# A two-layer-mixer trunk on one core: the first norm's modulation taken as stationary blocks by TensorE

## The chip, the cores and the metric

The kernel runs on one core of one Trainium2 chip. The metric is the device time of one execution in microseconds. An engine is named as in the profile: PE is TensorE, with PEld its weight loads, DVE is VectorE, ACT is ScalarE, POOL is GpSimd, SP issues the transfers.

## The reference

One decoder layer with a mixer and a feed-forward part, each behind an RMS norm that is scaled and shifted by a conditioning vector c. What matters here is the head of it:

```python
c_act = jax.nn.silu(c)
mod = c_act @ w_mod[l] + b_mod[l]                      # (1, 6 * 1024)
sh1, sc1, gt1, sh2, sc2, gt2 = [m[:, None, :] for m in jnp.split(mod, N_MOD, axis=-1)]
h = rms_norm(x, norm_mix[l]) * (1.0 + sc1) + sh1
p = h @ w_in[l]
p_a, p_b, p_c = jnp.split(p, [P_A, P_A + P_B], axis=-1)
```

Behind it stand three kinds of heads on slices of p (a spatial gating unit, a gated linear recurrence, a delta-rule recurrence), the output projection, a second norm with sh2 and sc2, and a convolutional GLU of width 2816. The model width is 1024, the sequence 1024, all in f32.

## The kernel before

Channels lie on the 128 partitions (8 k tiles of the width), positions along the free axis in two halves of 512. A product in f32 precision is made as three products of rounded parts: each weight and each activation is split into a high part, a cast by ACT (L228), and a low part, the difference, by DVE or POOL (L229); then PE multiplies high by high, high by low and low by high.

The stage in question is the first norm of the first half, the part of `trunk` under the tile pool `st`. c goes through silu into `cs` (8 columns, L189 to L191). The squares of the 8 x tiles are summed into `sacc`; PE sums that over partitions with `ones` as the moving operand (`pss`), DVE makes the reciprocal root (`rsqrt`, 13 tiny operations), PE spreads it over the partitions (`pb`) and ACT copies it to `rb`.

The modulation is 12 groups of 512 outputs. The order of w_mod's columns is such that groups 0 to 3 hold shift and scale of the first norm, each group for two k tiles of h. A group's weights come as four blocks `wm` of 512 KB, with two k tiles each. In groups 0 to 3 the eight k tiles are shared: ACT scales k tiles 0 to 3 by their column of `cs` and POOL adds them (`mod_ap`, into the first `mb`); DVE scales and adds k tiles 4 to 7 (`mod_v`, into the second `mb`). `mod_fin` then lets PE sum both `mb` over the partitions, in 4 + 4 matmuls with an `mb` slice as stationary operand and one column of ones as moving operand, into a PSUM tile `pm`; DVE adds the bias (`modc`) and makes the gain (`sg1`, named `sg` in the profile).

Of each group's two tiles of h, DVE multiplies x by gain and `rb` (`h_hi`; for k tiles 4 to 7 POOL has multiplied by `rb` already, `xr`), ACT adds the shift and rounds to the high part (h00h to h07h), DVE takes the low part (`h_lo`, h00l to h07l). Three weight tiles of w_in (`ws`, split into wh_s and wl_s) are multiplied as their h tiles come: `prod(k1, i1)` makes all products up to k tile k1 of the first i1 weight tiles, each once, into `pf`. The rest of w_in follows in later lines with `load_w` and `gemm`.

The order on each engine is that of the program's text wherever the wrapper `Ordered` is on (`V.on` and its like). It is on for DVE, ACT and POOL through this stage, and for PE around `mod_fin` and `prod` (`TON`). SP issues transfers in the text's order; each waits until its buffer is free (6 buffers of `wm`, 3 of the raw w_in tile). Behind the stage comes a row of small operations on `spt` (a softplus of 3 columns by series, L457 to L476), mostly on POOL, ACT's two parts of it behind h07h in ACT's queue.

Of the kernel before, what the change touches and what calls it, by code (L numbers as in the profile page):

```python
# [10 lines left out]
F32 = mybir.dt.float32  # L11
F32R = mybir.dt.float32r
I32 = mybir.dt.int32
AF = mybir.ActivationFunctionType
ALU = mybir.AluOpType
# [3 lines left out]
P = 128  # L19
D = 1024  # L20
S = 1024
H = 512
# [32 lines left out]
NF2 = 3  # L55
NT2, NTB, _ = 7, 9, 5
NWR, NWL, NH = 3, 2, 16
NAP, NXV, NFIRST, TON, XRO = (4, 4, 4, 4), 4, 3, True, ((4, 4), (4, 6), (6, 8), (8, 8))
VPIN = 0
ENG = {'s2':'G','KB1': 'V',  # L60
 'S1': 'V',
# [88 lines left out]
def trunk(ctx: ExitStack, tc: tile.TileContext, xT, wmod, w_in, w_out, w_up, w_down,  # L150
          par, const, sgu_ln, sgu_wT, sgu_b, lora, g2w, lruw, outT):
    nc = tc.nc
    V, A, G, T = (Ordered(tc, e) for e in (nc.vector, nc.scalar, nc.gpsimd, nc.tensor))
# [70 lines left out]
    def eng(key, d):  # L224
        return {"V": V, "G": G, "A": A}[ENG.get(key, d)]

    def split(src, hi, lo, e=None):
        A.copy(hi, src)  # L228
        (e or V).tensor_tensor(lo, src, hi.bitcast(F32), ALU.subtract)  # L229
# [100 lines left out]
    with tc.tile_pool(name="st", bufs=1, reuse_waits="tile") as st:  # L330
        xs, ws = [], []

        def mod_load(m):
            for k2 in range(KT // 2):
                wt = st.tile([P, 2, H], F32, tag="wm", name=f"wm{m}_{k2}", bufs=6)
                SY.dma_start(wt, wmod[m, k2])
                wm[m] += [wt[:, 0, :], wt[:, 1, :]]
            mb[m] = [st.tile([P, H], F32, tag=f"mb{i}", name=f"mb{m}{i}", bufs=2) for i in range(2)]

        def mod_ap(m):  # L340
            a = mb[m][0]
            for k in range(NAP[m]):
                A.activation(wm[m][k] if k else a, wm[m][k], AF.Copy, scale=cs[:, k:k + 1])
                if k:
                    G.tensor_tensor(a, a, wm[m][k], ALU.add)

        def mod_v(m, k0, k1):
            a = mb[m][1]
            for k in range(max(k0, NAP[m]), k1):
                if k == NAP[m]:  # L350
                    V.tensor_scalar(a, wm[m][k], cs[:, k:k + 1], None, ALU.mult)
                else:
                    V.scalar_tensor_tensor(a, wm[m][k], cs[:, k:k + 1], a, ALU.mult, ALU.add)

        def mod_fin(m):
            ps = mp.tile([P, H], F32, tag="m", name=f"pm{m}")
            for n, a in enumerate(mb[m]):
                for i in range(4):
                    T.matmul(ps[:, i:i + 1], a[:, i * P:(i + 1) * P], ones, start=(n == 0 and i == 0), stop=(n == 1),
                             skip_group_check=True)  # L360
            V.tensor_tensor(modc[:, 4 * m:4 * m + 4], ps[:, 0:4], col("b_mod", 4 * m, 4), ALU.add)
            V.scalar_tensor_tensor(sg1[:, 2 * m:2 * m + 2], modc[:, 4 * m + 1:4 * m + 4:2], 1.0,
                                   col("norm_mix", 2 * m, 2), ALU.add, ALU.mult)

        def w_load(i):
            raw, hi, lo = ws[i]
            SY.dma_start(raw, w_in[i].rearrange("p k c -> p (k c)"))

        def h_hi(k):
            x, sh = xs[k], modc[:, 2 * k:2 * k + 1]  # L370
            if k < NXV:
                V.scalar_tensor_tensor(x, x, sg1[:, k:k + 1], rb, ALU.mult, ALU.mult)
            else:
                V.tensor_scalar(x, x, sg1[:, k:k + 1], None, ALU.mult)
            A.activation(hs[k][0], x, AF.Identity, bias=sh)

        def h_lo(k):
            V.scalar_tensor_tensor(hs[k][1], xs[k], modc[:, 2 * k:2 * k + 1], hs[k][0].bitcast(F32),
                                   ALU.add, ALU.subtract)

        def xr(k0, k1):
            for k in range(k0, k1):
                G.tensor_tensor(xs[k], xs[k], rb, ALU.mult)

        wm, mb = [[] for _ in range(4)], [None] * 4
        hs = [htile(f"h0{k}") for k in range(KT)]
        acts[0] += hs
        for i in range(NFIRST):
            raw = wp.tile([P, 1024], F32, tag="wraw", name=f"wr_s{i}", bufs=NWR)
            hi = st.tile([P, 1024], F32R, tag=f"wsh{i}", name=f"wh_s{i}")  # L390
            lo = st.tile([P, 1024], F32R, tag=f"wsl{i}", name=f"wl_s{i}")
            ws.append((raw, hi, lo))
            first[i] = acp.tile([P, H], F32, tag="acc", name=f"pf{i}")

        done = [0] * NFIRST

        def prod(k1, i1):
            for k in range(k1):
                ah, al = hs[k]
                for i in range(min(i1, NFIRST)):  # L400
                    if done[i] == k:
                        hi, lo = (t.rearrange("p (k c) -> p k c", c=P)[:, k, :] for t in ws[i][1:])
                        T.matmul(first[i], hi, ah, start=(k == 0), stop=False)
                        T.matmul(first[i], hi, al, start=False, stop=False)
                        T.matmul(first[i], lo, ah, start=False, stop=(k == KT - 1))
                        done[i] += 1

        V.on = A.on = G.on = True
        sacc = st.tile([P, H], F32, name="sacc0")
        for k in range(KT):  # L410
            xk = st.tile([P, H], F32, tag=f"x{k}", name=f"x0{k}")
            SY.dma_start(xk, xT[k * P:(k + 1) * P, 0:H])
            sq = st.tile([P, H], F32, tag="sq", name=f"sqx{k}", bufs=2)
            A.activation(sacc if k == 0 else sq, xk, AF.Square)
            if k:
                V.tensor_tensor(sacc, sacc, sq, ALU.add)
            xs.append(xk)
        mod_load(0)
        mod_load(1)
        mod_ap(0)  # L420
        rb = sumsq_bcast([sacc], mp, st, "rb", "n10", 1)
        mod_v(0, 0, 8)
        w_load(0)
        mod_load(2)
        w_load(1)
        mod_load(3)
        if NFIRST == 3:
            w_load(2)
        SY.dma_start(cst, const[:, 0:C_ID])
        lraw = wp.tile([P, 1024], F32, tag="wraw", name="lraw", bufs=NWR)[:, 0:768]  # L430
        SY.dma_start(lraw, lora.rearrange("p a b -> p (a b)"))
        for m in range(4):
            if m < 3:
                mod_ap(m + 1)
                mod_v(m + 1, 0, 6)
            xr(*XRO[m])
            T.on = TON
            mod_fin(m)
            if TON:
                prod(2 * m, m)  # L440
            T.on = False
            h_hi(2 * m)
            h_hi(2 * m + 1)
            if m < 3:
                mod_v(m + 1, 6, 8)
            h_lo(2 * m)
            h_lo(2 * m + 1)
            if m < NFIRST:
                split(*ws[m], eng(f"s{m}", "V"))
        prod(KT, NFIRST)  # L450
        V.on = A.on = G.on = False

    r2 = r2s.enter_context(tc.tile_pool(name="r2", bufs=1, reuse_waits="tile"))
# [950 lines left out]
```

## Time and profile before

| what | value |
|---|---|
| median of 3 runs | 1389.36 us (1388.76 to 1389.72) |
| the profiled execution | 1389.59 us |
| its span | 1387.8 us |
| PE busy in the span | 1256.2 us (91%) |
| DVE, ACT, POOL busy | 914.4, 584.0, 413.3 us |
| PE busy, 30 to 62.2 us | 19.50 of 32.20 us |
| DVE busy, 30 to 62.2 us | 31.65 of 32.20 us |

A view by windows gives, for each stretch of the span, its length, the busy time of each engine with the number of instructions, then the granted clock of TensorE as a share of 2.4 GHz, the DMA share and GB/s. A timeline row is start, duration (of the whole row), engine, line, operation, tiles and count; in brackets the idle time ahead of it and what ended it. Line L146 is the wrapper `Ordered`, so rows of this stage are told apart by their tiles. Buffer numbers are left out: `wm` is any of its blocks. An f32 matmul has two records, so a row of x8 is four matmuls.

### The profile page before, as it was taken

Reading aid. Unit: us, or ns where it says so; the run is one execution under the profiler, and the core shown is the slowest. Engines: PE = TensorE matmul, PEld = TensorE weight load, DVE = VectorE, ACT = ScalarE, POOL = GpSimd, SP = SyncE. Lnnn points to the kernel's source line nnn. Section 1 sums busy time; section 2 is a strip of 40 time slices with the busy share of each in tenths; the row PEclk is TensorE's granted clock in tenths of the full one; section 3 lists DMA queues with packets and bytes.
Section 4 is the critical chain, followed back from the end, with each engine's and each line's share of the span. In section 5 each row is a group of like instructions: output and inputs, shape, how many; then the busy total and the mean of one; then the engine's idle time right before and its main releaser. Section 6 shows DMA issues by size and latency. Waiting matters only on the chain. (4 is left out here: it accounts for less than half of the span.)

```text
span 1387.8 us, 18658 instructions
## 1 busy us (share of the span) xinstructions
PE 1256.2 (91%) x6948; PEld 1025.9 (74%) x6948; DVE 914.4 (66%) x1624; ACT 584.0 (42%) x1008; POOL 413.3 (30%) x337
## 2 busy tenths in 40 slices
PE   2778999978898979989878999999999999999996
PEld 2566878667686867768656778888888888888885
DVE  7968776765668584567898766666666575332566
ACT  3454654854655366333444334343343342110231
POOL 5683423306124220023466433323333200000000
PEclk9999999979999988899989999999999999999998
DMA  6554161433314243385412322222222374321213
GB/s 225 189 168 121 35 168 52 113 126 97 83 51 109 65 124 107 116 272 188 137 45 84 100 91 84 91 84 91 74 71 91 109 261 133 93 76 51 82 54 121
DMA packets 87498, 153.89 MB, mean 111 GB/s; under 512 B 37616, under 2 KB 39280, under 8 KB 87408
## 3 DMA queue, kind: packets, MB, share of 16 engines
q1 hardware_dynamic: 87408, 152.71, 35.3%
q8 instruction: 54, 0.88, 0.3%
q14 instruction: 36, 0.29, 0.1%
HBM read 126.60 MB, written 26.08 MB: 110 GB/s over the span
## 5 line engine op out<-in xcount | busy, mean ns | idle before, releaser
L1246 DVE SCALAR_TENSOR_TENSOR x<-pd,modc,x 128x512 f32<-128x512 f32 x80 | 59.5, 748 | 83.4 <-PE pd L248 83.3
L1293 POOL TENSOR_TENSOR x<-x,rb_n 128x512 f32<-128x512 f32 x2 | 3.0, 1520 | 218.2 <-ACT rb_n L270 218.2
L287 POOL TENSOR_TENSOR macc<-macc,wm 128x512 f32<-128x512 f32 x35 | 46.8, 1338 | 68.1 <-ACT wm L285 66.0
L228 ACT CAST wh_wd<-wr_wd 128x768 fp32r<-128x768 f32 (+2 forms) x32 | 21.7, 677 | 93.6 <-PE pd L247 92.2
L229 POOL TENSOR_TENSOR wl_wo<-wr_wo,wh_wo 128x1024 fp32r<-128x1024 f32 x9 | 22.0, 2445 | 113.3 <-DVE O L774 57.6
L1224 POOL TENSOR_TENSOR u<-u,g 128x512 f32<-128x512 f32 x21 | 27.7, 1321 | 92.6 <-ACT g L1147 92.6
L229 DVE TENSOR_TENSOR wl_ug<-wr_ug,wh_ug 128x1024 fp32r<-128x1024 f32 x22 | 28.9, 1318 | 34.3 <-ACT wh_ug L228 34.3
L755 DVE TENSOR_SCALAR U<-q,rn 128x64 f32<-128x64 f32 x48 | 13.4, 279 | 48.3 <-PE q L743 41.1
L624 PE MATMUL pg<-KGd,KB 128*128 128x128 f32 x192 | 31.1, 307 | 7.5 <-DVE KGd L609 5.0
L763 ACT COPY O<-q 128x64 f32<-128x64 f32 x48 | 10.1, 211 | 65.5 <-PE q L743 65.2
L228 ACT CAST wh_ug<-wr_ug 128x1024 fp32r<-128x1024 f32 x22 | 23.1, 1052 | 34.2 <-PE pA L1122 31.3
L743 PE MATMUL q<-SS,KGd 128*128 128x64 f32 x180 | 36.7, 287 | 0.0
L743 PE MATMUL q<-VV,SCd 128*128 128x64 f32 x192 | 35.0, 285 | 0.3
L1208 DVE TENSOR_TENSOR p<-p,pB 128x512 f32<-128x512 f32 x21 | 14.4, 685 | 31.0 <-PE pB L1123 31.0
L1147 ACT ACTIVATE g<-g 128x512 f32<-128x512 f32 x44 | 27.9, 634 | 14.8 <-DVE g L1142 14.8
L624 PEld LDWEIGHTS pg<-KGd,KB 128*128 128x128 f32 x192 | 27.2, 215 | 9.0 <-DVE KGd L609 5.7
L228 ACT CAST wh_wo<-wr_wo 128x1024 fp32r<-128x1024 f32 x16 | 16.7, 1047 | 38.8 <-PE po L247 30.9
L743 PEld LDWEIGHTS q<-VV,SCd 128*128 128x128 f32 x192 | 29.9, 202 | 4.1 <-ACT O L763 1.4
L1140 DVE SCALAR_TENSOR_TENSOR g<-pA,pr,g 128x511 f32<-128x511 f32 (+1 forms) x42 | 31.2, 742 | 2.4 <-ACT g L1138 2.2
L1140 DVE SCALAR_TENSOR_TENSOR g<-p,pr,g 128x511 f32<-128x511 f32 (+1 forms) x42 | 32.1, 764 | 0.9 <-ACT g L1138 0.9
L285 ACT ACTIVATE wm<-wm,cs 128x512 f32<-128x512 f32 x35 | 24.1, 718 | 15.3 <-DMA wm<-in_wmod_dram 9.3
L1201 POOL TENSOR_TENSOR wr_ug<-wr_ug,wr_uv 128x512 f32<-128x512 f32 x18 | 29.7, 1651 | 1.4
(5041 smaller groups left out, 4574.1 us busy)
## 6 DMA issues: line engine op xcount, KB each, us to landing
wm<-in_wmod_dram SPq DMA_DIRECT2D x48, 512.0 KB, 4.1
wr_ug<-in_w_up_dram SPq DMA_DIRECT2D x22, 512.0 KB, 3.6
wr_uv<-in_w_up_dram SPq DMA_DIRECT2D x22, 512.0 KB, 3.6
wr_g<-gd SPq DMA_DIRECT2D x22, 512.0 KB, 3.5
x<-in_xT_dram SPq DMA_DIRECT2D x32, 256.0 KB, 5.2
wr_wo<-in_w_out_dram SPq DMA_DIRECT2D x16, 512.0 KB, 4.3
wr_wd<-in_w_down_dram SPq DMA_DIRECT2D x16, 384.0 KB, 3.0
gd<-c SPq DMA_DIRECT2D x21, 256.0 KB, 2.0
```

Source lines behind the costliest of these rows:

```text
L228: A.copy(hi, src)
L229: (e or V).tensor_tensor(lo, src, hi.bitcast(F32), ALU.subtract)
L285: A.activation(acc if k == 0 else wt[:, j, :], wt[:, j, :], AF.Copy, scale=cs[:, k:k + 1])
L287: G.tensor_tensor(acc, acc, wt[:, j, :], ALU.add)
L624: T.matmul(pg[hh][:, c, :, :], KB[:, 4 * g + c, :, :].rearrange("p a b -> p (a b)"), KG[g][:, c, :, r_], start=True, stop=True)
L743: T.matmul(o, w, x, start=start, stop=True, skip_group_check=True)
L1140: V.scalar_tensor_tensor(g[:, d:H], src[:, 0:H - d], taps[2 - d], g[:, d:H], ALU.mult, ALU.add)
L1147: A.activation(g, g, AF.Silu)
L1201: eng("S4" + e, "G").tensor_tensor(g1, g1, v1, ALU.subtract)
L1208: V.tensor_tensor(self.p1, self.p1, psB, ALU.add)
L1224: eng("c22", "V").tensor_tensor(u3, u3, g1_, ALU.mult)
L1246: V.scalar_tensor_tensor(x, ps, modc[:, 40 + k:41 + k], x, ALU.mult, ALU.add)
```

## The change

In groups 0 to 3 PE takes blocks of w_mod itself. `mod_pe` uses a 128 x 128 block of `wm` as stationary operand and the fitting column of `cs` as moving operand, four matmuls for each k tile, all into the group's `pm`. Group 0 does so for all eight k tiles, the first four ahead of `pss` and the others behind `pb`. In groups 1 to 3 PE takes k tiles 4 to 7, and DVE scales and adds k tiles 0 to 3 into one `mb`, which PE adds with `ones` as before. `mod_ap` is gone, and with it all work of POOL and ACT on the blocks. POOL now multiplies all eight x tiles by `rb`, ACT multiplies them by the gain, and POOL takes the low parts of all three first weight tiles (before, DVE took two). `wm` has 8 buffers instead of 6. PE is in program order through the whole stage.

```diff
+        def mod_pe(m, k0, k1, end=False):
+            if m not in pms:
+                pms[m] = mp.tile([P, H], F32, tag="m", name=f"pm{m}")
+                fresh.add(m)
+            src = [(wm[m][k], cs[:, k:k + 1]) for k in range(k0, k1)]
+            if end and mb[m] is not None:
+                src.append((mb[m], ones))
+            for n, (w, x) in enumerate(src):
+                for i in range(4):
+                    T.matmul(pms[m][:, i:i + 1], w[:, i * P:(i + 1) * P], x, start=m in fresh,
+                             stop=end and n == len(src) - 1, skip_group_check=True)
+                    fresh.discard(m)
...
         def h_hi(k):
             x, sh = xs[k], modc[:, 2 * k:2 * k + 1]
-            if k < NXV:
-                V.scalar_tensor_tensor(x, x, sg1[:, k:k + 1], rb, ALU.mult, ALU.mult)
-            else:
-                V.tensor_scalar(x, x, sg1[:, k:k + 1], None, ALU.mult)
+            A.activation(x, x, AF.Copy, scale=sg1[:, k:k + 1])
             A.activation(hs[k][0], x, AF.Identity, bias=sh)
...
-        mod_ap(0)
-        rb = sumsq_bcast([sacc], mp, st, "rb", "n10", 1)
-        mod_v(0, 0, 8)
...
+        T.on = True
+        mod_pe(0, 0, 4)
+        rb = sumsq_bcast([sacc], mp, st, "rb", "n10", 1)
+        mod_pe(0, 4, 8, True)
+        mod_v(1, 0, 4)
+        xr(0, 4)
+        mod_fin(0)
         for m in range(4):
-            if m < 3:
-                mod_ap(m + 1)
-                mod_v(m + 1, 0, 6)
-            xr(*XRO[m])
-            T.on = TON
-            mod_fin(m)
-            if TON:
-                prod(2 * m, m)
-            T.on = False
             h_hi(2 * m)
             h_hi(2 * m + 1)
             if m < 3:
-                mod_v(m + 1, 6, 8)
+                mod_pe(m + 1, 4, 8, True)
             h_lo(2 * m)
             h_lo(2 * m + 1)
-            if m < NFIRST:
-                split(*ws[m], eng(f"s{m}", "V"))
+            if m < 3:
+                mod_fin(m + 1)
+                if m < 2:
+                    mod_v(m + 2, 0, 4)
+                split(*ws[m], eng(f"s{m}", "G"))
+                xr(*((4, 6), (6, 8), (8, 8))[m])
+                prod(2 * m + 2, m + 1)
         prod(KT, NFIRST)
```

PE's queue from its start, before: `pss` is first, and a group is two rows of four matmuls.

```order
L255 MATMUL pss_n_221<-ones,sacc_154 128x1 x4
L266 MATMUL pb_n_241<-ident,rsq_n_228 128x128 x4
L146 MATMUL pm_287<-ones,mb_202 128x1 x4
L146 MATMUL pm_287<-ones,mb_203 128x1 x4
L146 MATMUL pm_319<-ones,mb_212 128x1 x4
L146 MATMUL pm_319<-ones,mb_213 128x1 x4
L146 MATMUL pf_145<-h00h,wh_s_143 128x512
```

The same place after the change: 16 matmuls of group 0 stand ahead of `pss`, 16 behind `pb`, and group 1 has 16 + 4 ahead of the first product.

```order
L146 MATMUL pm_232<-cs,wm_0_194 128x1 x8
L146 MATMUL pm_232<-cs,wm_1_196 128x1 x8
L146 MATMUL pss_n_249<-ones,sacc_154 128x1 x4
L146 MATMUL pb_n_269<-ident,rsq_n_256 128x128 x4
L146 MATMUL pm_232<-cs,wm_2_198 128x1 x8
L146 MATMUL pm_232<-cs,wm_3_200 128x1 x8
L146 MATMUL pm_307<-cs,wm_2_206 128x1 x8
L146 MATMUL pm_307<-cs,wm_3_208 128x1 x8
L146 MATMUL pm_307<-ones,mb_292 128x1 x4
L146 MATMUL pf_145<-h00h,wh_s_143 128x512
```

Groups 2 and 3 have the same 16 + 4 matmuls ahead of 18 and of 48 products. ACT's queue at the end of the stage, before (the x tiles come scaled from DVE):

```order
L146 ACTIVATE h06h<-x_184,modc 128x512
L146 ACTIVATE h07h<-x_189,modc 128x512
L146 ACTIVATE spt<-pr 128x3
L228 CAST wh_r_610<-wr_r_608 128x1024
L146 ACTIVATE spt<-spt 128x3
```

And after, where ACT scales each x tile ahead of the h tile that is made from it:

```order
L146 ACTIVATE x_184<-x_184,sg_77 128x512
L146 ACTIVATE h06h<-x_184,modc 128x512
L146 ACTIVATE x_189<-x_189,sg_77 128x512
L146 ACTIVATE h07h<-x_189,modc 128x512
L146 ACTIVATE spt<-pr 128x3
L228 CAST wh_r_637<-wr_r_635 128x1024
L146 ACTIVATE spt<-spt 128x3
```

POOL's queue of the stage, after; before, 12 adds of blocks stood in it, four products by `rb` and the split of the third weight tile only.

```order
L146 TENSOR_TENSOR x_155<-x_155,rb_n_274 128x512
L146 TENSOR_TENSOR x_159<-x_159,rb_n_274 128x512
L146 TENSOR_TENSOR x_164<-x_164,rb_n_274 128x512
L146 TENSOR_TENSOR x_169<-x_169,rb_n_274 128x512
L146 TENSOR_TENSOR wl_s_144<-wr_s_142,wh_s_143 128x1024
L146 TENSOR_TENSOR x_174<-x_174,rb_n_274 128x512
L146 TENSOR_TENSOR x_179<-x_179,rb_n_274 128x512
L146 TENSOR_TENSOR wl_s_148<-wr_s_146,wh_s_147 128x1024
L146 TENSOR_TENSOR x_184<-x_184,rb_n_274 128x512
L146 TENSOR_TENSOR x_189<-x_189,rb_n_274 128x512
L146 TENSOR_TENSOR wl_s_152<-wr_s_150,wh_s_151 128x1024
```

All rows behind the stage stand in the same order as before on every engine, SP's from its first to its last.

## Rows read from the trace of the kernel before

**Rows 1.** Windows of the span, busy by engine, with granted clock before DMA share

```profile
30.00:62.20 32.20, 19.50 (x76) 16.19 (x77) 31.65 (x33) 12.00 (x17) 21.11 (x14) 0.98 0.62 231
...
24.85:30.13 5.28, 5.28 (x24) 5.19 (x24) 3.13 (x5) 3.04 (x5) 1.27 (x1) 1.00 0.46 117
49.52:53.94 4.42, 4.42 (x12) 3.40 (x13) 4.35 (x5) 0.93 (x2) 4.26 (x3) 1.00 0.44 118
53.94:60.90 6.96, 4.44 (x27) 3.57 (x25) 6.82 (x7) 2.38 (x3) 4.91 (x4) 0.99 0.01 4
61.77:67.60 5.83, 5.83 (x14) 4.57 (x15) 4.93 (x10) 3.41 (x6) 1.58 (x2) 0.50 0.30 90
67.60:75.24 7.64, 7.64 (x34) 5.96 (x32) 0.89 (x3) 2.27 (x4) 5.52 (x25) 1.00 0.46 144
65.72:86.02 20.30, 17.92 (x77) 14.14 (x76) 7.37 (x9) 9.09 (x17) 17.65 (x44) 0.95 0.66 210
...
546.00:556.00 10.00, 9.25 (x41) 8.75 (x41) 3.09 (x8) 6.68 (x12) 0.00 (x0) 0.50 0.00 0
```

**Rows 2.** Timeline of PE in the first stage

```profile
18.95 1.84 PE L255 MATMUL pss_n<-ones,sacc 128*128 128x1 f32 x8 [18.95 <-DVE sacc L146]
24.85 2.08 PE L266 MATMUL pb_n<-ident,rsq_n 128*128 128x128 f32 x8 [4.06 <-DVE rsq_n L146]
26.72 3.41 PE L146 MATMUL pm<-ones,mb 128*128 128x1 f32 x16
...
55.80 0.95 PE L146 MATMUL pm<-ones,mb 128*128 128x1 f32 x8
...
74.85 0.39 PE L405 MATMUL pf<-h07h,wl_s 128*128 128x512 f32 x1
```

**Rows 3.** Timeline of DVE, first stage and what follows it

```profile
13.25 0.17 DVE L191 TENSOR_TENSOR cs<-cs,pr 128x8 f32<-128x8 f32 x1
...
21.02 0.79 DVE L146 TENSOR_SCALAR rsq_n<-rsv_n 128x4 int32<-128x4 int32 x1
...
21.92 1.24 DVE L146 TENSOR_SCALAR rsq_n<-rsv_n 128x4 f32<-128x4 f32 x1
...
24.63 0.16 DVE L146 SCALAR_TENSOR_TENSOR rsq_n<-rsq_n 128x4 f32<-128x4 f32 x1
...
62.19 0.15 DVE L146 TENSOR_TENSOR modc<-pm,pr 128x4 f32<-128x4 f32 x1
...
86.05 1.22 DVE L572 TENSOR_TENSOR_SCAN cc<-scanm,sg 128x512 f32<-128x512 f32 x1 [5.75 <-POOL sg L570]
```

**Rows 4.** Timeline of ACT at the end of the first stage

```profile
63.79 0.70 ACT L146 ACTIVATE h07h<-x,modc 128x512 fp32r<-128x512 f32 x1
```

**Rows 5.** Timeline of POOL behind the first stage

```profile
65.72 1.17 POOL L146 TENSOR_SCALAR spt<-spt 128x3 f32<-128x3 f32 x1 [4.00 <-ACT spt L146]
...
85.40 0.62 POOL L570 TENSOR_SCALAR sg<-sg 128x512 f32<-128x512 f32 x1
```

**Rows 6.** Groups of equal instructions, 12 to 66 us: count, busy us, mean ns, idle before

```profile
L146 POOL TENSOR_TENSOR mb<-mb,wm 128x512 f32<-128x512 f32 x12 | 18.0, 1496 | 20.7 <-ACT wm L146 20.1
...
L146 DVE SCALAR_TENSOR_TENSOR mb<-wm,cs,mb 128x512 f32<-128x512 f32 x12 | 11.7, 972 | 0.3
...
L146 ACT ACTIVATE wm<-wm,cs 128x512 f32<-128x512 f32 x12 | 7.7, 706 | 0.0
L146 POOL TENSOR_TENSOR x<-x,rb_n 128x512 f32<-128x512 f32 x4 | 5.6, 1429 | 0.0
...
L146 ACT CAST wh_s<-wr_s 128x1024 fp32r<-128x1024 f32 x3 | 3.1, 1028 | 0.0
...
L146 POOL TENSOR_TENSOR wl_s<-wr_s,wh_s 128x1024 fp32r<-128x1024 f32 x1 | 2.6, 2553 | 2.0 <-ACT wh_s L146 2.0
```

**Rows 7.** Groups of PE instructions, 540 to 556 us

```profile
L743 PE MATMUL q<-VV,SCd 128*128 128x64 f32 x16 | 4.8, 398 | 0.1
```

**Rows 8.** DMA issues on the page: count, KB each, median us to landing

```profile
wm<-in_wmod_dram SPq DMA_DIRECT2D x48, 512.0 KB, 4.1
```

More of the change, by code (lines that the diff above doesn't have):

```diff
@@ L57 @@
 NWR, NWL, NH = 3, 2, 16
-NAP, NXV, NFIRST, TON, XRO = (4, 4, 4, 4), 4, 3, True, ((4, 4), (4, 6), (6, 8), (8, 8))
+NFIRST = 3
 VPIN = 0
@@ L334, in mod_load @@
             for k2 in range(KT // 2):
-                wt = st.tile([P, 2, H], F32, tag="wm", name=f"wm{m}_{k2}", bufs=6)
+                wt = st.tile([P, 2, H], F32, tag="wm", name=f"wm{m}_{k2}", bufs=8)
                 SY.dma_start(wt, wmod[m, k2])
                 wm[m] += [wt[:, 0, :], wt[:, 1, :]]
[L338 to L345, printed above, removed]
@@ L347, in mod_v @@
         def mod_v(m, k0, k1):
[L348 to L351, printed above, removed]
-                else:
-                    V.scalar_tensor_tensor(a, wm[m][k], cs[:, k:k + 1], a, ALU.mult, ALU.add)
-        def mod_fin(m):
[L356 to L360, printed above, removed]
+            for k in range(k0, k1):
+                if k == 0:
+                    mb[m] = st.tile([P, H], F32, tag="mb", name=f"mb{m}", bufs=2)
+                    V.tensor_scalar(mb[m], wm[m][k], cs[:, k:k + 1], None, ALU.mult)
+                else:
+                    V.scalar_tensor_tensor(mb[m], wm[m][k], cs[:, k:k + 1], mb[m], ALU.mult, ALU.add)
@@ L361, in mod_fin @@
+        def mod_fin(m):
+            ps = pms[m]
             V.tensor_tensor(modc[:, 4 * m:4 * m + 4], ps[:, 0:4], col("b_mod", 4 * m, 4), ALU.add)
@@ L383, in xr @@
                 G.tensor_tensor(xs[k], xs[k], rb, ALU.mult)
-        wm, mb = [[] for _ in range(4)], [None] * 4
+        wm, mb, pms, fresh = [[] for _ in range(4)], [None] * 4, {}, set()
         hs = [htile(f"h0{k}") for k in range(KT)]
@@ L426, in trunk @@
         mod_load(3)
-        if NFIRST == 3:
-            w_load(2)
+        w_load(2)
         SY.dma_start(cst, const[:, 0:C_ID])
@@ L444, in trunk @@
             if m < 3:
-                mod_v(m + 1, 6, 8)
+                mod_pe(m + 1, 4, 8, True)
             h_lo(2 * m)
             h_lo(2 * m + 1)
-            if m < NFIRST:
-                split(*ws[m], eng(f"s{m}", "V"))
+            if m < 3:
[5 more added lines that the diff above has]
+                prod(2 * m + 2, m + 1)
         prod(KT, NFIRST)
+        T.on = False
         V.on = A.on = G.on = False
```

## The prediction

> **What bounds the kernel now.** The change touches only the first norm, so I read that stage first, then what leaves it. From 30 to 62.2 us DVE is busy 31.65 of 32.20 us and PE 19.50 [rows 1]: there DVE is the limit, because it sums half of the modulation, scales x and splits weights. PE stands behind it: its small matmuls with `ones` run in bits of four and eight [rows 2]. The last of the four modulation groups reaches `modc` at 62.19 [rows 3]. Behind that hang ACT's h06h and h07h, then the two `spt` activations [rows 4], then a chain of small operations on POOL that starts at 65.72 and goes on without a real pause (17.65 us busy of 20.30) to `sg` at 85.40 [rows 1, 5]. DVE waited 5.75 us for exactly that and goes on at 86.05 [rows 3]. PE's last first-stage product starts at 74.85 [rows 2]. So what the change is worth is read from one moment: when the fourth `modc` can be computed. All instructions behind the stage stand in the same order on all five engines before and after; so I take the shift of that moment to reach the end one to one.
>
> **The change, part by part.** Removed: 12 adds on POOL (1496 ns each), 16 ACT scalings (12 of the `wm` kind at 706 ns), and on DVE 16 of the 972 ns kind become 12 [rows 6]; DVE also loses the scaling of x (to ACT, with POOL's product by `rb` before it) and two of three weight splits (to POOL). Added: 60 matmuls of one column on PE, 92 instead of 32. With this DVE has nothing left that fills the stage; the question is PE, which now works in program order and must do all of it before each group of h tiles.
>
> The price of such a matmul: eight of them in a row (16 records, an f32 matmul has two) took 3.41 us from 26.72, so 0.426 each; four (8 records) took 0.95 us from 55.80, so 0.24 (I use 0.25) [rows 2]. The difference is the clock: before 53.94 PE is at 1.2 GHz (that column of the view has no reading until its first change, so I go by the spacing), then 2.4 GHz until 60.90, 1.2 GHz (0.50) until 67.60, then 2.4 [rows 1]. The 512-column products take 5.83/14 = 0.42 us at the lower level (I use 0.43) and 7.64/34 = 0.225 at the upper [rows 1].
>
> Which level will hold? 5.28 us of unbroken small matmuls from 24.85 did not end in the upper clock; 4.42 us and 5.83 us of 512-column products did (49.52 to 53.94, 61.77 to 67.60) [rows 1]. And much later, from 546 to 556, f32 matmuls of 64 columns fill 9.25 of 10 us and the clock stays at 0.50 throughout [rows 1, 7]. So I take 1.2 GHz for the new matmuls wherever no run of 512-column products goes ahead. The Trainium skill ("TensorE: Matmul & The Clock Gate", Part 1, the HAM clock gate) says otherwise: sustained activity releases the clock, as a matter of time and not of the number of matmuls. By that rule the long new stretch would run at 2.4 GHz; the stretch at 546 does not agree, and the case is a rival below.
>
> Now PE's list, on the axis of the profiled execution:
> - First half of group 0: from `cs` (13.25 + 0.17, say 13.5 [rows 3]) 16 × 0.426 = 6.8, to 20.4 (a 512 KB block lands 4.1 us after its issue [rows 8], and these are asked for before any other weights). It stands ahead of `pss`, which began at 18.95 [rows 2]; so `pss` is 1.45 late and ends at 22.2.
> - DVE's rsqrt chain took from 20.79 to 24.79, with two tiny operations stretched to 0.79 and 1.24 us (0.16 is usual) [rows 2, 3] while POOL's adds ran. Those adds are gone. If the stretching goes too (about 1.7 us), `pb` starts at 24.6; if not, at 26.2. Nearest to the row's own operations without it is the first; with a little for gaps I take 24.85, as before.
> - `pb` 1.87 (24.85 to 26.72 [rows 2]); second half of group 0, 6.8, to 33.5; group 1 (16 + 4), 8.5, to 42.0; six products 2.7, to 44.7; group 2, 8.5, to 53.2.
> - Eighteen products: the upper clock comes after 4.42 or 5.83 us of them, so 4.42 + 7.7 × 0.225 = 6.2 or 5.83 + 4.4 × 0.225 = 6.8; I take 6.6, to 59.8.
> - Group 3: after its first rise the upper clock lasted 7 us (53.94 to 60.90 [rows 1]) though small matmuls and waits filled much of it. From a rise at about 58.4 that reaches to 65, so 20 matmuls at 0.25, 5.0, to 64.8. At the lower level it would be 8.5.
>
> Does PE wait for anything in between? The nearest case is POOL's split of the first weights, needed at about 42.5. `modc` of group 0 is ready at 33.6; ACT's four operations on x and h and the cast (1028 ns [rows 6]) take to 38, the split 2.55 us (2553 ns [rows 6]), to 40.4; POOL's four products by `rb` (1429 ns each [rows 6]) are done by 33.3. That leaves 2 us. The blocks of groups 2 and 3 that wait for PE's reading are asked for at 30 to 42 and wanted 10 us later or more, against 4.1 us to land [rows 8]. So PE is unbroken from 24.85 on, and is the limit.
>
> The fourth `modc` then comes at 64.8 against 62.19: **2.6 us later**. Behind it ACT now does four operations, each pair dependent, about 2.85 us (0.71 each [rows 6]) plus 0.35 for `modc` and its gain; before, h07h ended at 63.79 + 0.70, 2.3 us after `modc` [rows 3, 4]. That is another **1.0 us**. POOL's chain starts 3.6 us later. PE's own 48 remaining products: 5.8 us at the lower level (13.6 of them), then 34.4 × 0.225 = 7.7, so to 78.3 against 75.24, 3.1 late: the two meet as before. Sum: +3.6 us.
>
> The profiled execution took 1389.59 us (span 1387.8 and 1.8 around it), the median of the runs shown is 1389.36; from the median, **1393.0**. What a measurement of this kernel can tell from no change is about 0.2%, 2.8 us; the sum lies a little beyond.
>
> **Rivals.**
> - *The clock rises in the small matmuls* (faster). If they raise it as the products from 49.52 did, 4.42 us after the unbroken run begins at 24.85, that is at 29.3. Group 0 then ends at 31.8, group 1 at 36.8; PE waits for the first split to 38.7; group 2 ends at 44.8, the eighteen products at 49.0, group 3 at 54.0. `modc` comes 8.2 us earlier, less the 1.0 on ACT: -7.1, **1382**. It decides from the point where a small matmul in the second half of group 0 costs 0.25 instead of 0.43. For it: the stretch at 24.85 is one of 5.28 us only, and the new one, to 42, is over three times as long; against it, that stretch and the ten us at 546 [rows 1, 7]. It is also what the rule of the Trainium skill's page "TensorE: Matmul & The Clock Gate", Part 1, would give.
> - *It rises around the six products* at 42 to 44.8 (no change). It decides if group 2's first matmul already costs 0.25. Group 2 at 0.25 is 3.5 us shorter, the eighteen products 2.4, so `modc` at 58.9 and -2.3 in all, **1387**; if it rises only within group 2, between that and +2.7. The same verdict would come if the first chain gains and the clock rises early in the eighteen.
> - *It falls before group 3* (slower still). Then group 3 is 8.5 us, to 68.3, +7.1, **1396.5**; with the rsqrt chain still stretched (+1.5), 1398.
> - That the change does not do what it says is no rival: the order shows the matmuls and the moved operations.
>
> **How the numbers follow.** Forecast +2.8 to +6: 0.58 (1393.0). Falls before group 3: 0.12. No change, by the second rival or by delay taken up behind the stage: 0.20. Clock up in the small matmuls: 0.10. So faster 0.10, same 0.20, slower 0.70. The range goes down to 1388.5, into the second rival, and up to 1398, the end of the third; about 0.2 is left out, most of it the first rival.
>
> **What would show it.** In the trace after: PE without idle from about 25 us to the end of its first-stage products; the one-column matmuls of groups 0 to 2 at 0.43 us each; DVE with long idle before each `modc`, ended by PE; the fourth `modc` at 64 to 66 and POOL's `spt` at 68.5 to 70.5; the interval between any two later landmarks unchanged. Small matmuls at 0.25 in groups 0 and 1 would make it wrong to the fast side; PE waiting for `wl_s` or for a block, or a `modc` at 68, to the slow side.

## The result

The changed kernel takes 1396.64 us (median of 13 runs, 1390.54 to 1400.49), the kernel before in the same comparison 1387.93 (13 runs, 1383.97 to 1390.93): a ratio of 1.0052, 95% interval 1.0033 to 1.0071. It is slower by 4.6 to 9.9 us; I had forecast +3.6. The sign and the engine were right, the size was not: the larger part of the loss lies where I had put 1.45 us.

Its profiled execution is the shortest of the 13: 1390.54 us, 0.95 us above the profiled one of before. Read against that one profile the change seems to cost a microsecond. Why this is a wrong reading is the main thing below.

### The profile page after: what moved, and what is told of

It reads as the page before. It is cut to its first block, busy times and chain, and to the rows that moved or that the text cites. A ratio compares the mean times of both kernels' runs of the same rounds, so it can differ in the third digit from the quotient of the medians.

```text
span 1388.7 us, 18862 instructions
## 1 busy us (share of the span) xinstructions
PE 1278.3 (92%) x7068; PEld 1049.7 (76%) x7068; DVE 881.6 (63%) x1610; ACT 579.0 (42%) x1000; POOL 403.5 (29%) x331
## 5 line engine op out<-in xcount | busy, mean ns | idle before, releaser
L146 PE MATMUL pm<-cs,wm 128*128 128x1 f32 x160 | 31.1, 329 | 12.5 <-DMA wm<-in_wmod_dram 12.5
L146 PEld LDWEIGHTS pm<-cs,wm 128*128 128x128 f32 x160 | 31.5, 304 | 12.8 <-DVE sacc L146 12.5
L762 ACT COPY O<-q 128x64 f32<-128x64 f32 x48 | 10.1, 210 | 64.7 <-PE q L742 64.4
```

Of the source, the lines that this page charges most:

```text
L146: return lambda *a, **k: self.tc.keep_in_program_order(f(*a, **k))
```

## The profile after

The page of the changed kernel (busy time of each engine, then the group of the one-column matmuls on `wm`). PE is 22 us busier than before, DVE 33 us less busy; the 160 records are 80 one-column matmuls on `wm`, all new, while those with `ones` went from 32 to 12.

```profile
PE 1278.3 (92%) x7068; PEld 1049.7 (76%) x7068; DVE 881.6 (63%) x1610; ACT 579.0 (42%) x1000; POOL 403.5 (29%) x331
...
L146 PE MATMUL pm<-cs,wm 128*128 128x1 f32 x160 | 31.1, 329 | 12.5 <-DMA wm<-in_wmod_dram 12.5
```

PE's timeline in the stage (start, duration, then the instruction; in brackets the idle time ahead of it and what ended it). Lines between, products and the small matmuls with `ones`, are left out.

```profile
12.54 6.96 PE L146 MATMUL pm<-cs,wm 128*128 128x1 f32 x32 [12.54 <-DMA wm<-in_wmod_dram]
19.36 1.84 PE L146 MATMUL pss_n<-ones,sacc 128*128 128x1 f32 x8
23.64 2.07 PE L146 MATMUL pb_n<-ident,rsq_n 128*128 128x128 f32 x8 [2.44 <-DVE rsq_n L146]
25.51 13.65 PE L146 MATMUL pm<-cs,wm 128*128 128x1 f32 x64
...
43.44 6.82 PE L146 MATMUL pm<-cs,wm 128*128 128x1 f32 x32
...
57.84 3.62 PE L146 MATMUL pm<-cs,wm 128*128 128x1 f32 x32
```

PE starts at 12.54, when the first block of w_mod has landed, 7.0 us after SP asked for it. `cs` had been ready since 4.3. The rows of DVE and of SP:

```profile
4.16 0.17 DVE L191 TENSOR_TENSOR cs<-cs,pr 128x8 f32<-128x8 f32 x1
```

```profile
5.45 6.05 SPq L336 DMA_DIRECT2D wm<-in_wmod_dram  x8
```

From 23.64 to the end of the stage PE has no idle, and a one-column matmul takes 13.65/32 = 0.43 us until the products of the second and third group have run; the last 16 take 0.23 each. That is the list of the prediction, 1.1 us earlier up to the third `modc` and 2.4 at the fourth. DVE now waits for PE ahead of every `modc` (its timeline; [rows 3] had the fourth at 62.19 without a wait, and `cc` at 86.05):

```profile
32.37 0.16 DVE L146 TENSOR_TENSOR modc<-pm,pr 128x4 f32<-128x4 f32 x1 [6.03 <-PE pm L146]
40.90 0.16 DVE L146 TENSOR_TENSOR modc<-pm,pr 128x4 f32<-128x4 f32 x1 [4.46 <-PE pm L146]
52.00 0.16 DVE L146 TENSOR_TENSOR modc<-pm,pr 128x4 f32<-128x4 f32 x1 [6.42 <-PE pm L146]
62.40 0.16 DVE L146 TENSOR_TENSOR modc<-pm,pr 128x4 f32<-128x4 f32 x1 [5.96 <-PE pm L146]
87.09 1.23 DVE L571 TENSOR_TENSOR_SCAN cc<-scanm,sg 128x512 f32<-128x512 f32 x1 [6.83 <-POOL sg L569]
```

ACT's four dependent operations behind the fourth `modc`, first and last of them, and then POOL's first `spt` operation, which stood at 65.72 [rows 5]:

```profile
62.85 0.72 ACT L146 ACTIVATE x<-x,sg 128x512 f32<-128x512 f32 x1 [6.62 <-DVE sg L146]
...
64.98 0.72 ACT L146 ACTIVATE h07h<-x,modc 128x512 fp32r<-128x512 f32 x1
```

```profile
66.92 1.16 POOL L146 TENSOR_SCALAR spt<-spt 128x3 f32<-128x3 f32 x1 [8.23 <-ACT spt L146]
```

From the fourth `modc` to `spt` it is 4.52 us, before 3.53: ACT's part is the 1.0 us of the prediction. All in all `cc` stands 1.04 us later than in the profile of before. The medians differ by 8.7. Two theories: **stage**, the loss is in the first norm and the profile of before is not like its other runs; **behind**, it arises later, where PE's clock falls at one wait or another.

## The experiments

### More profiles of the two kernels, unaltered

> The changed kernel once more, unaltered, for a second profile. Its 13 runs so far lie between 1390.5 and 1400.5 us (median 1396.6), and the profiled one is the fastest of them: there the fourth modc came at 62.40 us and the scan cc at 87.09, 0.2 and 1.04 us later than before. Theory 'stage': what the other runs have in excess lies in the first-norm stage, because the clock rises later there or falls before group 3; then a profiled run of 1396 us shows the fourth modc at 65 to 68, group 3 at 0.43 us a matmul, and cc later by the same 3 to 6 us. Theory 'behind': the stage ends within 0.5 us of 62.4 in every run, cc within 0.5 us of 87.1, and the excess arises after 100 us, in stretches where PE gets the lower clock in one run and not in another. A profiled run near 1391 tells nothing apart.

The changed kernel again: 1396.47 us (11 runs, 1390.64 to 1402.98), ratio 1.0059 (1.0036 to 1.0081). The profile is now of a run of 1396.47 us. PE's small matmuls of groups 2 and 3, and the end of the stage on DVE:

```profile
43.09 3.91 PE L146 MATMUL pm<-cs,wm 128*128 128x1 f32 x32
...
55.14 4.83 PE L146 MATMUL pm<-cs,wm 128*128 128x1 f32 x32
```

```profile
61.71 0.16 DVE L146 TENSOR_TENSOR modc<-pm,pr 128x4 f32<-128x4 f32 x1 [7.70 <-PE pm L146]
...
86.51 1.23 DVE L571 TENSOR_TENSOR_SCAN cc<-scanm,sg 128x512 f32<-128x512 f32 x1 [5.75 <-POOL sg L569]
```

Here the clock rose at the end of the six products (group 2: 0.24 us a matmul), fell again, rose late in the eighteen products and fell within group 3 (0.30 us a matmul). The second rival and a part of the third took place in one run and cancelled: the fourth `modc` is 0.7 us earlier than in the first profile, the whole run 6 us longer. "Stage" as it was worded ahead of this run (`modc` at 65 to 68) failed, and "behind" held but for 0.2 us: the stage of the changed kernel is steady, and what separates its own runs lies behind it. That leaves "stage" as I put it above, with the oddity in the profile of before.

> The kernel before once more, unaltered, for a second profile and as a control of the comparison. Four profiles of the changed kernel and its variants lie within +0.2 to +2.4 us of the one profile of before at 100 us, and at +0.9 to +12.4 at the end; what is added in between stands in stretches where PE runs at 1.2 GHz in one and at 2.4 GHz in the other. Theory 'lot': at most of PE's waits behind the stage it is a matter of chance whether the clock falls; then this profile of before also shows low stretches at places where the first did not (326, 367, 671, 781 us), and its span lies anywhere from 1382 to 1393. Theory 'kernel': those low stretches belong to the changed kernel; then before shows none at 326, 367 and 671 us here either. Ratio to before: 1.000 within 0.002.

> The kernel before a third time, for its profile alone. As for the second: theory 'lot' expects low clock at some of 326, 367, 671 and 781 us, theory 'kernel' at none of them.

The kernel before against itself gave 1.0016 (0.9992 to 1.0039). Its second profile, PE first, then DVE:

```profile
13.10 1.84 PE L255 MATMUL pss_n<-ones,sacc 128*128 128x1 f32 x8 [13.10 <-POOL STd L490]
19.35 2.08 PE L266 MATMUL pb_n<-ident,rsq_n 128*128 128x128 f32 x8 [4.41 <-DVE rsq_n L146]
```

```profile
2.87 0.27 DVE L193 TENSOR_SCALAR omu<-pr 128x11 f32<-128x11 f32 x1 [2.87 <-DMA pr<-in_par_dram]
...
5.07 0.17 DVE L191 TENSOR_TENSOR cs<-cs,pr 128x8 f32<-128x8 f32 x1
26.50 0.15 DVE L146 TENSOR_TENSOR modc<-pm,pr 128x4 f32<-128x4 f32 x1
...
56.67 0.15 DVE L146 TENSOR_TENSOR modc<-pm,pr 128x4 f32<-128x4 f32 x1
...
80.48 1.23 DVE L572 TENSOR_TENSOR_SCAN cc<-scanm,sg 128x512 f32<-128x512 f32 x1 [6.84 <-POOL sg L570]
```

This stage ends 5.5 us earlier than in [rows 3], and so does that of the third profile:

```profile
57.05 0.15 DVE L146 TENSOR_TENSOR modc<-pm,pr 128x4 f32<-128x4 f32 x1
...
81.05 1.23 DVE L572 TENSOR_TENSOR_SCAN cc<-scanm,sg 128x512 f32<-128x512 f32 x1 [6.83 <-POOL sg L570]
```

What was different in the first one stands at its very start. DVE's timeline there, and the last of POOL's series of memsets:

```profile
2.78 10.12 DVE L193 TENSOR_SCALAR omu<-pr 128x11 f32<-128x11 f32 x1 [2.78 <-DMA pr<-in_par_dram]
2.86 10.05 DVE L195 TENSOR_SCALAR hw<-pr 128x3 f32<-128x3 f32 x1
...
13.25 0.17 DVE L191 TENSOR_TENSOR cs<-cs,pr 128x8 f32<-128x8 f32 x1
```

```profile
11.92 0.96 POOL L490 MEMSET STd<- 128x1024 f32 x1
```

Five operations on 3 to 11 columns took 10 us: they ended when POOL's memsets ended (12.9), and `cs`, the sum of squares and `pss` came late with them. All eight profiles of the changed kernel and its variants have `cs` by 5.1 us; whether that is chance or comes of the change, no run shows. Against an ordinary start of before (`cc` at 80.48 and 81.05, mean 80.8) the change costs 5.7 to 6.3 us at `cc`, not 1.04.

That the first profile of before took no longer in all than the others (span 1387.8; 1392.3 and 1388.4 for the second and third) goes back to places behind the stage. Windows of three profiles at two such places; the column ahead of the DMA share is the granted clock (first profile of before, second profile of before, changed kernel):

```profile
210.00:225.00 15.00, 14.50 (x254) 11.38 (x254) 5.59 (x13) 11.84 (x24) 2.48 (x4) 1.00 0.13 38
320.00:336.00 16.00, 13.23 (x82) 11.19 (x80) 11.52 (x22) 8.37 (x16) 11.43 (x11) 1.00 0.33 99
```

```profile
210.00:225.00 15.00, 14.76 (x108) 11.28 (x108) 4.90 (x11) 8.80 (x18) 1.42 (x2) 0.61 0.12 36
320.00:336.00 16.00, 14.09 (x69) 12.19 (x69) 8.76 (x18) 8.22 (x15) 10.90 (x10) 0.79 0.34 99
```

```profile
210.00:225.00 15.00, 14.41 (x254) 11.23 (x253) 6.47 (x15) 11.83 (x24) 2.48 (x4) 1.00 0.15 55
320.00:336.00 16.00, 14.12 (x66) 12.05 (x65) 8.40 (x19) 7.50 (x14) 10.75 (x10) 0.79 0.31 94
```

In one run of the same kernel the clock falls to its lower level there, in the other not: "lot" held, "kernel" did not. The second profile of before is 4.5 us ahead of the first at 110 us and 4.5 behind it at the end, 9 us over the rest of the run, with a mean granted clock of 0.947 against 0.957. I put these 9 us down to such places; only two of them are shown. They hide a difference of the stage in a single run. So from here on I read the stage from the trace (`cc`) and the time from medians.

### Group 0 alone undone

```diff
-        mod_pe(0, 0, 4)
-        rb = sumsq_bcast([sacc], mp, st, "rb", "n10", 1)
-        mod_pe(0, 4, 8, True)
+        (the four pss matmuls)
+        mod_v(0, 0, 2)
+        mod_pe(0, 4, 6)
+        rb = rstd_bcast(pss, mp, st, "rb", "n10", 1)
+        mod_v(0, 2, 4)
+        mod_pe(0, 6, 8, True)
```

> The changed kernel with group 0 alone undone in part: DVE takes the first four k tiles of group 0 (as in the groups 1 to 3), and pss stands ahead of all small matmuls on PE. Theory 'first group': in three profiles of before with an ordinary start (one of them with a few more POOL operations far behind) pss runs at 13.1 us, the first modc comes at 26.5 to 26.9, the fourth at 56.7 to 57.1 and cc at 80.5 to 81.6; in the profile that I predicted from, five small DVE operations took 10 us and the stage stood 5.5 us later. So the change costs 6 us at cc, and it does so in group 0: 16 small matmuls ahead of pss. Then here the first modc comes at 25 to 26.5, the fourth at 55 to 57 instead of 62.4, cc at 80 to 81.5, and the median falls by 5 to 8 us from the changed kernel's 1396.5, to within 0.25% of before. Rival 'small matmuls in all groups': group 0 is short, but the rest keeps PE's list at 0.43 us and only half of it (3 us) is won at the fourth modc, because PE or the splits wait elsewhere. Rival 'lot': the median stays within 2 us of 1396.

Ratio 1.0007 (0.9989 to 1.0025): level with before. PE and DVE:

```profile
13.07 1.84 PE L146 MATMUL pss_n<-ones,sacc 128*128 128x1 f32 x8 [13.07 <-POOL STd L494]
...
18.26 2.06 PE L146 MATMUL pb_n<-ident,rsq_n 128*128 128x128 f32 x8
```

```profile
25.26 0.16 DVE L146 TENSOR_TENSOR modc<-pm,pr 128x4 f32<-128x4 f32 x1 [3.77 <-PE pm L146]
...
54.95 0.16 DVE L146 TENSOR_TENSOR modc<-pm,pr 128x4 f32<-128x4 f32 x1 [5.01 <-PE pm L146]
...
79.74 1.23 DVE L576 TENSOR_TENSOR_SCAN cc<-scanm,sg 128x512 f32<-128x512 f32 x1 [5.74 <-POOL sg L574]
```

With `pss` back at 13 us and half of group 0 on DVE the fourth `modc` and `cc` come some 7.4 us earlier, and the loss is gone, although groups 1 to 3 are as the change made them. "First group" holds, as far as the whole loss fits in the interval; "lot" would have left the ratio at that of the changed kernel, 1.0052, which lies outside. The run joins two edits, the order (`pss` first) and the amount (PE makes 20 small matmuls in group 0 instead of 32); a later run tells them apart.

### One microsecond on POOL in the kernel before

```diff
     G.memset(a_, 1.0 / 19)
+    spx = cp.tile([P, 3], F32, name="spx")
+    G.memset(spx, 0.0)
+    for n in range(2):
+        G.tensor_tensor(spx, spx, s2_, ALU.mult)
+        G.tensor_scalar(spx, spx, 1.0, None, ALU.add)
```

> The kernel before with five more small operations on POOL in the spt chain (a scratch tile, nothing reads it): 1.0 to 1.2 us more on POOL ahead of sg, so cc at 87.1 instead of 86.05, as in the changed kernel; nothing else of the change. Theory 'offset': what the change costs behind the stage comes from its 1 us of delay at cc alone, because it shifts the later waits against the clock's decisions; then this kernel, too, has a median 6 to 9 us above before's. Theory 'lot' or any other source: the median rises by 1 us, within 0.2% of before.

Ratio 1.0085 (1.006 to 1.011), +11.8 us, with `cc` at 81.58, only 0.8 us later. This seemed to say that a microsecond at `cc` can cost ten. It does not: from 850 to 1350 us PE is busy throughout at the upper clock in both, and does fewer matmuls here (second profile of before, then this kernel):

```profile
850.00:1350.00 500.00, 500.00 (x2207) 414.01 (x2207) 285.44 (x425) 162.52 (x262) 92.17 (x69) 1.00 0.31 98
```

```profile
850.00:1350.00 500.00, 500.00 (x2178) 408.50 (x2177) 277.90 (x417) 159.98 (x258) 91.80 (x68) 1.00 0.31 98
```

1.3% fewer, and from 850 us to the end the run loses 7.6 us to the second profile of before. No other kernel here shows this. The new tile of 12 bytes a partition moves the tiles behind it in SBUF; that this is the cause is a guess. The run settled nothing about `cc`, so I repeated it on the tile that was there:

```diff
+    for n in range(2):
+        G.memset(a_, 1.0 / 19)
+        G.tensor_tensor(a_, a_, s2_, ALU.mult)
+        G.tensor_scalar(a_, a_, 1.0 / 17, None, ALU.add)
     G.memset(a_, 1.0 / 19)
```

> The kernel before with six more small operations on POOL in the spt chain, this time on the tile that is there already (the first steps of the series are done twice more and overwritten): 1.0 to 1.3 us more ahead of sg. The earlier form of this with a tile of its own had every matmul of the last 500 us some 1.5% slower, 7.6 us in all, which had nothing to do with POOL. Theory 'stage, one to one': cc at 81.5 to 82.2 and the median 1 us above before's, within 0.2% of it, and no drift from 800 to 1350 us. Theory 'offset' (a microsecond of delay at cc turns more of the later waits into falls of the clock): median 3 to 9 us above before's.

Ratio 1.0016 (0.9999 to 1.0034), +2.2 us, and no drift. Its profile has the late start again (`omu` 10.23 us), with `cc` at 87.46 against 86.05 of the other such profile, +1.4. One to one within the interval; an effect of 6 to 9 us from the offset is out, and so are the extra POOL operations as the source of the drift.

### The scaling of x back on DVE

```diff
-            A.activation(x, x, AF.Copy, scale=sg1[:, k:k + 1])
+            V.tensor_scalar(x, x, sg1[:, k:k + 1], None, ALU.mult)
```

> One part undone alone: the scaling of x by sg1 stands on DVE again (POOL's product by rb and all matmuls stay as in the changed kernel). ACT then has two operations behind each modc instead of four. My reckoning of ACT's part (+1.0 us): h07h ends at 64.7 instead of 65.7, POOL's chain starts at 65.9 instead of 66.92, cc at 86.1 instead of 87.1, and the median is 1.0 us lower, 1395.6, which by itself lies within the scatter. Rival: DVE's two scalings are as dependent as ACT's, and nothing moves (within 0.2 us at cc).

From the fourth `modc` to POOL's `spt` it is now 2.73 us (62.66 to 65.39) instead of 4.52: ACT's part is there. But `cc` came at 89.18, and the ratio stayed at 1.0052 (1.0032 to 1.0071). The edit also moved a DVE operation: the last `spt` operation, which waits for POOL, now stands ahead of `wl_v`; DVE's timeline:

```profile
73.58 0.16 DVE L146 SCALAR_TENSOR_TENSOR spt<-spt 128x3 f32<-128x3 f32 x1 [6.08 <-POOL spt L146]
73.66 1.22 DVE L229 TENSOR_TENSOR wl_v<-wr_v,wh_v 128x1024 fp32r<-128x1024 f32 x1
```

In the changed kernel `wl_v` runs at 68.21. With it came the load of `wm` behind it on SP, and ACT, which wants that block, waited 11.53 us. The part was undone and something else done; only the first reading counts.

### Six k tiles on DVE, and the spt block ahead

```diff
-                mod_pe(m + 1, 4, 8, True)
+                mod_pe(m + 1, 6, 8, True)
```

(and `mod_v(.., 0, 6)` in place of `mod_v(.., 0, 4)`)

> In groups 1 to 3 DVE takes six of eight k tiles instead of four, PE two: 24 one-column f32 matmuls fewer. Theory 'stage' (PE's small matmuls at 0.43 us are the limit and their length is what costs): each group is 3.4 us shorter, less a wait of about 1.5 us for the first weight split on POOL; the fourth modc comes at 55 to 57 instead of 62.4, cc at 80.5 to 82, and the median falls by 5 to 7 us, to about 1390, below or at the kernel before (1387.9) only if the scatter goes too. Theory 'behind': the fourth modc comes earlier by as much, but the median falls by less than 3 us or in no relation to it, and the scatter of some 10 us stays. Third: DVE becomes the limit (six times 0.78 us and two of 0.75 us for h, 6.2 us a group) and the fourth modc moves by under 3 us.

Ratio 1.0026 (1.0007 to 1.0044). The fourth `modc` at 60.98, only 1.4 us earlier, `cc` at 85.75. PE has 24 matmuls fewer and waits instead, for DVE's sum of group 2:

```profile
49.31 1.87 PE L146 MATMUL pm<-ones,mb 128*128 128x1 f32 x8 [4.92 <-DVE mb L146]
```

The third expectation held: the limit went to DVE, which begins that sum only when the `modc` before it is done.

The second of the pair writes the whole spt block ahead of `mod_pe(0, 0, 4)`, its last three operations behind `mod_fin(0)`.

> The changed kernel with the spt block (softplus of lru_lambda: two small ACT operations, some 25 small POOL ones, two on DVE) written before the stage's first matmuls instead of behind the stage; POOL is idle from 13.0 to 26.4 us there. If POOL's chain from 66.92 to sg (86.43) sets cc, as I read it, 9.6 us leave it, and the next that sg waits for is ACT's sg at 81.14: cc at 82 to 83 instead of 87.1, and if a shift of the stage's end reaches the end one to one, the median falls by 4 to 5 us, to 1392. Rival: PE or DVE behind cc have slack that takes it up: cc moves by 4 to 5 us and the median by under 2.

Ratio 1.0027 (1.0008 to 1.0045), `cc` at 85.63: 0.9 to 1.5 us earlier, not 4 to 5. The ratio fell by more than that, 0.0025 to 0.0032 (some 4 us), but the intervals overlap. POOL's list had a second limit under the first, a memset that PE's products release:

```profile
74.69 0.74 POOL L483 MEMSET lol<- 128x768 f32 x1 [18.06 <-PE pf L146]
```

It waits for one of PE's last first-stage products, and these start as late as 75.53. Nearly ten microseconds of POOL work came off the chain (66.92 to 76.55) and bought about one.

### Versions that use this

The first has `pss` ahead of PE's first half of group 0, six k tiles on DVE with some of them written ahead of the `modc` before, and spt early.

> The changed kernel with three edits: pss ahead of the first half of group 0 on PE (so DVE's rsqrt chain runs beside small matmuls, pb 2.2 us earlier), six of eight k tiles on DVE in groups 1 to 3 with part of them written ahead of the wait for the modc before (so PE does not wait 4.9 us for mb as in the run with six tiles), and the spt block ahead of the stage. Theory 'stage': the fourth modc comes at 53 to 57 instead of 62.4, PE's last first-stage product starts at 65 to 69 instead of 74.6, cc at 77 to 80, and the median falls by 7 to 9 us from the changed kernel's, to 1387 to 1390, equal to before or below. Rival: a later resource takes the gain (the loads of weights that SP issues when the buffers come free, ACT's copies): cc moves by 4 us or less, median 1392.

Fourth `modc` 53.47, `cc` 79.25, ratio 0.9983 (0.9961 to 1.0004). Its first `modc` tells order and amount apart, for here `pss` is first (13.25), but PE still makes all 32 small matmuls of group 0:

```profile
30.49 0.16 DVE L146 TENSOR_TENSOR modc<-pm,pr 128x4 f32<-128x4 f32 x1 [5.61 <-PE pm L146]
```

That row stood at 32.37 in the changed kernel and at 25.26 in the group-0 run. So of 7.1 us at the first `modc` the order is worth 1.9, and the other 5.2 go with the amount (12 matmuls fewer, 0.43 us each).

The second takes the half of group 0 to DVE as above, and splits DVE's sums 2 + 4 around `mod_fin`:

```diff
+                if m < 2:
+                    mod_v(m + 2, 0, 2)
                 mod_fin(m + 1)
                 if m < 2:
-                    mod_v(m + 2, 0, 4)
+                    mod_v(m + 2, 2, 6)
```

> As the run before, and in groups 1 to 3 DVE takes six of eight k tiles (two of them written ahead of the modc before, four behind it), and the spt block stands ahead of the stage. The earlier combination had its fourth modc at 53.5, cc at 79.25 and a median 1.3 us under before's; DVE's in-order wait for the third modc (44.3 to 49.5 us) and PE's 1.7 us wait for POOL's last split are mended here and group 0 is 5 us shorter. Theory 'stage': the fourth modc at 46 to 49, cc at 72 to 75, the median 6 to 8 us below before's (ratio 0.9945 to 0.9955). Rival: the loads that SP issues as buffers come free, or POOL's list behind the stage, set cc: cc not under 77, median 2 to 3 us below before's.

Ratio 0.9962 (0.9944 to 0.998): 2.8 to 7.8 us faster than before, and some 0.9% faster than the changed kernel. DVE's timeline:

```profile
51.80 0.16 DVE L146 TENSOR_TENSOR modc<-pm,pr 128x4 f32<-128x4 f32 x1 [1.93 <-PE pm L146]
...
72.76 1.23 DVE L578 TENSOR_TENSOR_SCAN cc<-scanm,sg 128x512 f32<-128x512 f32 x1 [5.17 <-POOL sg L576]
```

The fourth `modc` came 3 to 6 us later than I expected, since PE still waits 2.35 us for POOL's first weight split and 1.73 us for a sum; `cc` is 8.0 us earlier than before's.

### The late start itself

```diff
-    V.tensor_scalar(omu, col("rwkv_mu", 0, 11), -1.0, 1.0, ALU.mult, ALU.add)
+    A.activation(omu, col("rwkv_mu", 0, 11), AF.Copy, scale=-1.0, bias=1.0)
```

(and the same for the other small ones and the first of the two on `cs`, in the kernel before)

> The kernel before with its first six small DVE operations of one form (TENSOR_SCALAR: omu, hw, ha, hbx, hka, oka) and the first of the two on cs moved to ACT, nothing else. Two of five profiles of before and its variants with a longer POOL list had these operations last 10 us, from 2.8 to 12.9 us, as long as POOL's series of memsets, and their stage 5.5 us later; three had them done by 5 us. Theory 'late start': what DVE waits for there is POOL, and runs of before are a mixture of both starts; then here the profile has cs by 5 us, cc at 80 to 81, and the median is 1 to 4 us below before's with fewer runs in its upper part. Rival: the late start comes from elsewhere (the first loads), then it is still among these runs, and the median is within 1 us of before's.

`cs` at 3.23 us, `cc` at 81.16, ratio 0.999 (0.9968 to 1.0012). The time did not move. The start is ordinary in this profile, as it was in three of five profiles without the edit, so one profile proves no cure; and the medians of before are not raised measurably by late starts. Either they are rare outside profiles or their 5.5 us are lost and found again behind the stage; which, I can't tell from these runs. The two profiled runs that had one took 1389.59 and 1392.98 us, 1.7 above and 1.4 below the median of their sets, and two runs with a scatter of 7 to 15 us decide nothing. If late starts were frequent, before's median would hold them, and the 5.7 to 6.3 us of the change would be too much.

### All kernels together

`cc` less the 80.8 us of an ordinary start of before, beside what the ratio makes of 1388 us; each interval is about 2.5 to 3.5 us either way.

| kernel | cc, us later | ratio | time, us |
|---|---|---|---|
| changed, first and second set | +6.3, +5.7 | 1.0052, 1.0059 | +7.2, +8.2 |
| scaling on DVE | +8.4 | 1.0052 | +7.2 |
| six k tiles on DVE | +5.0 | 1.0026 | +3.6 |
| spt early | +4.8 | 1.0027 | +3.7 |
| group 0 halved | -1.1 | 1.0007 | +1.0 |
| first combination | -1.5 | 0.9983 | -2.4 |
| second combination | -8.0 | 0.9962 | -5.3 |
| before, POOL longer (first form) | +0.8 | 1.0085 | +11.8 |
| before, POOL longer (second form) | +1.4 (against 86.05) | 1.0016 | +2.2 |
| before, small operations on ACT | +0.4 | 0.999 | -1.4 |

But for the first form of the longer POOL list, most of whose loss lies in the last 540 us, the times follow `cc` one to one within their intervals; the second combination stands at their edge (-8.0 against -2.8 to -7.8). Theory "stage" holds. "Behind" explains the scatter of runs, not the difference of the medians; two microseconds of it are within the uncertainty and I leave them open.

## Why the prediction was right, and its size wrong

- **PE unbroken, small matmuls at 0.43 us.** Right: no idle from 23.64, 0.43 us each in groups 0 and 1 in both profiles of the changed kernel. After 15.2 us of unbroken one-column matmuls (25.51 to 40.73) the lower clock still held; it rose behind 512-column products, 3.9 us into the eighteen in the first profile, at the end of the six in the second. The Trainium skill ("TensorE: Matmul & The Clock Gate", Part 1, the HAM clock gate) has the warm-up as a matter of time of activity, not of a number of matmuls; these 15.2 us do not agree. The first rival did not occur.
- **PE's list.** The steps between the four `modc` were 8.5, 11.1 and 10.4 us; by my list 8.5, 11.2 and 11.6. In the first profile the clock rose 3.9 us into the eighteen products, half a microsecond under my lower bound, and held for group 3; in the second profile it rose earlier and fell earlier, and the end differed by 0.7 us.
- **"So `pss` is 1.45 late": the step that failed, a term of the sum with the wrong size.** I took `pss` at 18.95 from [rows 2] as what the kernel does. `pss` waits for the sum of squares, and in that one execution this was late because five small DVE operations had taken 10 us. In an ordinary start `pss` runs at 13.10, and 16 matmuls ahead of it put it at 19.36: **6.3 us, not 1.45**. The rsqrt chain gives some of it back, for its stretching is gone as I took it (2.33 us from 21.25 to 23.58), so `pb` is 4.3 us late. The first `modc` is 5.9 late: the second half of group 0 takes 3.4 us more than the eight matmuls of before, of which 1.9 were free there, because `modc` waited for DVE. The group-0 run takes back order and amount together. The row that should have made me ask was there: `cs`, eight columns, only at 13.25 in [rows 3], though its input had landed at 2.78.
- **The start of the new matmuls.** I had 13.5, from `cs`; they start at 12.54, and that it is so near is luck. `cs` is there at 4.3, and PE waits for the first block of w_mod, which takes 7.0 us to land where I took 4.1, the median of all 48 blocks in [rows 8]. A block that lands by 6.3 us would let all 16 end before 13.1 and cost `pss` nothing; that is an estimate from 0.43 us each, and no run here tries it.
- **The fourth `modc` +2.6.** Against the profile that I had, +0.2; against ordinary starts, 62.40 and 61.71 less 56.67 and 57.05, some 4.7 to 5.7. My number lies between the two for no good reason. The places that I named, `modc` at 64 to 66 and `spt` at 68.5 to 70.5, were missed: 62.40 and 66.92.
- **ACT +1.0.** Measured 0.99.
- **One to one to the end.** In medians, within their intervals or, once, at the edge. In single runs not at all.
- **"The median is like the profiled run", said without saying it.** I set the profile beside a median of three runs 0.2 us off and took it for typical. Its time was; its first 20 us were not, and its luck behind the stage paid for them.
- **The range.** 1396.64 us lies in it only because it reaches up to the third rival, which I had at 1396.5. That rival did not occur as a whole: the clock held through group 3 in the first profile and fell within it in the second, and neither fourth `modc` comes near its 68.3. That the number is so near its price is luck.
- **Slips that move nothing.** [rows 6] counts 12 operations of 972 ns on DVE, which become 9, and not 16 that become 12; in the first rival group 2 ends at 45.0 by its own steps, not at 44.8.

## What to carry to other kernels

One profiled execution is one draw: before a term rests on when something starts, ask of the operation ahead of it whether its duration fits its size, and where it does not, do the sum with the ordinary duration too. Work put first on an in-order engine costs what stands behind it there, so the small product that everything waits for goes ahead of the bulk; but count the bulk too, for here the order was worth 1.9 us and the amount 5.2. And a long list on another engine that seems to set the end may have a second limit just under it: follow what its next operation waits for once the list is shorter.

## What the runs showed that I had not expected

- Small DVE operations of one form (TENSOR_SCALAR, 3 to 11 columns) beside a series of POOL memsets of 0.95 us: done within one or two of them in three profiles of before and its variants, held to the end of the series (10.1 and 10.2 us) in two. The Trainium skill ("SBUF — State Buffer", Who interferes with whom) has the two engines share a port pair that the first to issue holds for the whole of its instruction; that the other waits through a whole series of them it does not say. The three profiles agree with that, the two do not; no run here shows the port itself.
- With a tile of 12 bytes more a partition PE did 1.3% fewer matmuls at the same clock for 500 us, 7.6 us in all, and without that tile but with as many POOL operations it did not. Why is open.
- Runs of one kernel in one comparison lie 7 to 15 us apart, and their profiles differ in the places where the clock falls; a difference of 5 us needs medians of a dozen runs, and a single pair of profiles can show it with the wrong size.
